# Context statistics, state products and reloaded results in other places of a two-layer DiT kernel, and the rotation on VectorE

## The chip, the cores and the metric

The kernel runs on one core of a Trainium2 chip. The metric is device time in microseconds (us) for one execution. TensorE (PE) does matrix products, VectorE (DVE), ScalarE (ACT) and GpSimd (POOL) do everything else on tiles, and SyncE (SP) issues most of the transfers between HBM and the on-chip memory. Each engine takes its own instructions in the order in which they were queued; between engines there are semaphores.

## The reference, cut to what matters

Two layers act on 512 rows `x` and 256 context rows `ctx`, each 2048 wide. Layer 0 (pooling and latent attention) isn't touched by the change. Layer 1 ("odd") is:

```
h, hc = rmsnorm(x)*(1+scale)+shift, rmsnorm(ctx)*(1+scale_c)+shift_c
mq,mk,mv,mo,mg,mz,aq,ak,av,az = split(h @ w_in)       # the same split of hc @ w_in for the context
state = mlstm_scan(context)                           # matrix memory: sums of w * v x k over the context
hm    = mlstm_scan(rows, state), forward and backward
ym    = rmsnorm(hm) * sigmoid(mo) * silu(mz)          # 4 heads of 256
q, k  = rope_2d(aq), rope_2d(ak)
ya    = window_attention(q, k, v, kc, vc, sink) * silu(az)   # 16 heads of 64, window 128, plus context
y     = concat(ym, ya) @ w_out
x     = x + gate * y ;  result = rmsnorm(x)
```

## The kernel before, in words

Everything is transposed: a tile holds 128 channels (partitions) by 512 rows or 256 context rows, so a 2048-wide value is 16 such tiles ("chunks", `j` = 0 to 15). Every operand of a product is split into a high and a low part in a rounded float type (`split`, line 107: a cast on ACT, line 108, then a subtraction on VectorE, line 109), and each product is three matmuls: high by high, high by low, low by high. Weights come in quarters of 128x1024 (`kq` = 0 to 3): `load_w` (line 111) issues the transfer from SP into one of three `wraw` buffers and splits it into four `wh` and four `wl` buffers, which is room for two quarters. `tmode` (line 299) and `kmode` (line 313) issue the matmuls of a quarter.

The order on the engines comes from a scheduling pass of the framework: it simulates the engines, and gives each one the earliest instruction in the source that is ready in that simulation. So the place in the source is a priority, not a position. Inside the blocks marked `manual_schedule` the order on PE is the order of the source, and some steps are marked `high_priority`.

The stages that the change touches:

- **Row statistics and the second layer's inputs** (lines 905 to 985). `stats1(v)` adds the squares of all chunks over the partitions with small matmuls (line 267 by way of `stat_mm`), takes the reciprocal root (`rstd_col`, lines 241 to 245), and spreads it with matmuls (`rows`, line 260). `h_chunk` (line 278) then makes the high and low parts of one chunk: a scaled product (line 289), an ACT step (line 291) and a VectorE step (line 292). For the rows these are the `HX` tiles (`hxh`, `hxl`), for the context the `HC` tiles (`hch`, `hcl`). In the source `stats1(1)` and the 16 context chunks stand ahead of both query groups of matrix memory (`x_group_t(6)` and `(7)`, 96 matmuls of 512 columns each, which read `HX` alone). The next group, which makes the first values and the gates, is the first that reads `HC`.
- **Context state** (lines 1199 to 1246). For each of the 4 heads `ctx_state` is a generator with two steps for each direction: scale the values (line 1219, VectorE) and split them (`wvh`, `wvl`); then six matmuls (line 1228) and a split of their result. One call starts it when a head's values are stored; two more calls come inside the next projection group, after its quarters 0 and 2. The background work that runs here on VectorE (`ada_vec_steps`, line 187) takes 128x512 blocks of a modulation weight from HBM.
- **Matrix memory** (line 1276 to 1435) makes eight result chunks (`z1d` 0 to 7, in HBM).
- **Windowed attention** (line 1440 to the end of the loop over heads). Its matmuls are interleaved by hand: a generator `fillers` yields one 512-column matmul at a time from the remaining projections (`w_proj(1)` to `w_proj(3)`: a query group and a gate group each) and then from the first three groups of the output projection (`out_steps`); `run(n)` takes n of them. `PRE`, `PRE2`, `PRE3` say how many are taken at the start, and `RATE` how many for each step of the attention. `wq_split` rotates a query tile (`do_rope`, line 329: a shuffle and a product on VectorE, a product on GpSimd at line 337, a sum on VectorE) and splits it. `Softmax.heads` (line 1511) takes scores for two heads: the masked maximum (line 1527), its scaled form against the sink (line 1528), the exponential (line 1529); `end` divides. `w_values` transposes the weights (line 1640), splits them (`wph`, `wpl`) and multiplies by the values (lines 1650 and 1651).
- **The result chunks** come back from HBM as `Z` tiles: `z_load(j)` (line 1558) loads two, casts them on VectorE (line 1563) and subtracts on GpSimd (line 1564). Their buffers lie in the same place as the `HX` tiles, whose pool is closed just before. All loads for the first output group stand inside `out_steps(0)`.

Of the kernel before, what the change touches and what calls it, by code (L numbers as in the profile page):

```python
# [8 lines left out]
F32 = mybir.dt.float32  # L9
F32R = mybir.dt.float32r  # L10
# [28 lines left out]
def tile_hybrid_dit(ctx: ExitStack, tc: tile.TileContext, ts: dict, out: bass.AP, dbg=None, upto=99):  # L39
# [286 lines left out]
        DM.dma_start(t, ts["rope"])  # L326
        return t[:, 0, :], t[:, 1, :]

    def do_rope(ps, r, tmp):

        sw = tmp("rsw", NX)
        t1 = tmp("rt1", NX)
        with tc.high_priority():
            V.stream_shuffle(sw, ps[:, :NX], SWAP)  # L334
            V.tensor_tensor(t1, ps[:, :NX], rope[0], op=ALU.mult)
        t2 = tmp("rt2", NX)
        G.tensor_tensor(t2, sw, rope[1], op=ALU.mult)
        V.tensor_tensor(r[:, :NX], t1, t2, op=ALU.add)

    def rtmp(pool, bufs=1):  # L340
        return lambda name, n: pool.tile([P, n], F32, name=name, tag=name, bufs=bufs)
# [597 lines left out]
    ezx.close()  # L939
    ehx, ehc, eht = (ExitStack() for _ in range(3))  # L940
    hxp = opool(ehx, "hx", side="right")
    HX = [(hxp.tile([P, NX], F32R, name=f"hxh{j}"), hxp.tile([P, NX], F32R, name=f"hxl{j}")) for j in range(KC)]
    bg.finish()
    stats1(0)

# [27 lines left out]
    hcp = opool(ehc, "hc", side="right")  # L973
    HC = [(hcp.tile([P, NC], F32R, name=f"hch{j}"), hcp.tile([P, NC], F32R, name=f"hcl{j}")) for j in range(KC)]
    htp = opool(eht, "htp")
    stats1(1)
    for j in range(KC):
        h_chunk(j, x1[j], ssq1, 12, 1, *((None, HC[j][i]) for i in range(2)), Ring(htp, 2), (1,))
    for i in range(2):
        for b, px in enumerate(x_group_t(G_MQ + i)):  # L980
            q = htp.tile([P, NX], F32, name="mqt", tag="mqt", bufs=2)
            S.mul(q, px, M_SCALE)
            G.dma_start(qxd[2 * i + b], q)
# [215 lines left out]
    def mv_group(h, state):  # L1199
        px, pc = new_px(2), new_pc()  # L1200
        pv = [px[b // 2][:, 256 * (b % 2) : 256 * (b % 2) + 256] for b in range(4)]
        for kq in range(4):
            w = load_w(odw[1 + h, kq])
            kcs = range(4 * kq, 4 * kq + 4)
            bg.step(2)
            kmode(pv, w, kcs, HX, kq == 0, kq == 3, 2)
            bg.step(3)
            kmode([pc[:, b, :] for b in range(2)], w, kcs, HC, kq == 0, kq == 3, 2)
            if kq % 2 == 0:
                next(state, None)  # L1210
        vx_store(h, [p_.rearrange("p (a b) -> p a b", b=256) for p_ in px])
        return vc_store([pc])
# [26 lines left out]
    for kq in range(4):  # L1239
        w = load_w(odw[5, kq])  # L1240
        bg.step(2)
        tmode(px, [pc[:, b, :] for b in range(2)], w, range(4 * kq, 4 * kq + 4), HX, HC, kq == 0, kq == 3)
        if kq % 2 == 0:
            next(state, None)
    bg.finish()
    ea.close()
# [210 lines left out]

    def wq_split(src):
        rr = ap2.tile([P, NX], F32, name="wrr", tag="wrr", bufs=1)
        do_rope(src, rr, rtmp(ap2))  # L1460
        res = []
        for a in range(2):
            own, oth = slice(64 * a, 64 * a + 64), slice(64 - 64 * a, 128 - 64 * a)
            q = ap2.tile([P, NX], F32R, name="wq", tag="wq", bufs=8)
            S.copy(q[own, :], rr[own, :])
            V.tensor_tensor(q[oth, :], rr[own, :], q[own, :], op=ALU.subtract)  # L1466
            res.append(q)
        return res
# [12 lines left out]
    def w_proj(i):  # L1481

        for g in (G_AQ + i, G_AZ + i):
            px = new_px2()
            if g < G_AZ:
                qs[i] = []
            else:
                zg[i] = ap2.tile([P, 2, NX], F32, name="wzg", tag="wzg", bufs=2)
            for kq in range(4):
                w = load_w(odw[g, kq])  # L1490
                kcs = range(4 * kq, 4 * kq + 4)
                for b in range(2):
                    yield from steps(px, w, kcs, (b,), HX, kq == 0, kq == 3)
                    if kq == 3 and g < G_AZ:
                        qs[i] += wq_split(px[b])
                    elif kq == 3:
                        S.activation(zg[i][:, b, :], px[b], AF.Silu)

    def w_bounds(nb):
        b0, b1 = max(0, nb - 1), min(4, nb + 2)  # L1500
# [2 lines left out]
    class Softmax:  # L1503
# [7 lines left out]
        def heads(self, pair):  # L1511
            i, nb = self.i, self.nb
            g = i // 2
            b0, b1, nl = w_bounds(nb)
            nk = nl + NC
            mk = (msk[:, P:], msk, msk, msk3)[nb]
            qq = slice(nb * P, (nb + 1) * P)
            ss_ = [new_w2() for _ in pair]
            for a, s in zip(pair, ss_):
                q = qs[i][a][:, qq]  # L1520
                for n, K in enumerate((KHw[g], KLw[g])):
                    T.matmul(s[:, 512 - nl : 512], q, K[:, b0 * P : b1 * P], start=n == 0, stop=n == 1)  # L1522
                    T.matmul(s[:, 512:768], q, K[:, NX:], start=n == 0, stop=n == 1)  # L1523
            for a, s in zip(pair, ss_):
                pr = wt("wpr_", 640)
                mx = tiny.tile([P, 1], F32, name="wm1", tag="wm1", bufs=4)
                V.tensor_tensor_reduce(pr[:, :nk], s[:, 512 - nl : 768], mk[:, :nk], 1.0, -3e38, ALU.add, ALU.max, mx)
                V.scalar_tensor_tensor(self.nmx[:, a : a + 1], mx, -A_SCALE, nsink[:, 4 * i + a : 4 * i + a + 1], op0=ALU.mult, op1=ALU.min)
                S.activation(pr[:, :nk], pr[:, :nk], AF.Exp, bias=self.nmx[:, a : a + 1], scale=A_SCALE, accum_out=self.ssm[:, a : a + 1])
                self.prs.append(pr)  # L1530

# [15 lines left out]
    def out_steps(g, px):  # L1547

        for kq in range(4):
            n = 4 - 2 * (kq == 3)  # L1550
            if g == 0:
                for j in range(4 * kq, 4 * kq + n, 2):
                    z_load(j)
            w = load_w(ts["od_out"][g, kq])
            yield from steps(px, w, range(4 * kq, 4 * kq + n), range(2), Z, kq == 0, False)
        ends.append((px, w[2:]))

    def z_load(j):
        raw = wp.tile([P, 1024], F32, name="wraw", tag="wraw", bufs=3)
        for i in range(2):  # L1560
            DM.dma_start(raw[:, 512 * i : 512 * i + 512], z1d[j + i])
            h, l = Z[j + i]
            V.tensor_copy(h, raw[:, 512 * i : 512 * i + 512])  # L1563
            G.tensor_tensor(l, raw[:, 512 * i : 512 * i + 512], h, op=ALU.subtract)

    def fillers():

        nonlocal Z, ezf
        for i in range(1, 4):
            yield from w_proj(i)  # L1570
        ehx.close()
        ezf = ExitStack()
        zp = opool(ezf, "zp1", side="right")
        Z = [(zp.tile([P, NX], F32R, name=f"z1h{j}"), zp.tile([P, NX], F32R, name=f"z1l{j}")) for j in range(KC)]
        pxs.append(new_px2())
        yield from out_steps(0, pxs[0])
        for g in (1, 2):
# [1 line left out]
            pxs.append([t[:, :512], t[:, 512:]])  # L1579
            yield from out_steps(g, pxs[g])  # L1580

    PRE, PRE2, PRE3, RATE, RATE_END = 16, 8, 20, 9.5, 13
    Z = ezf = None
    pxs, ends = [], []
    fill = fillers()

# [182 lines left out]
        stat_mm(p6[:, :2], ssq2[:, sl], 2, D, True, False)  # L1769
        finish(sl, out_evac(7, px, sl), p6)  # L1770
    eF.close()
    ezf.close()
    esP.close()


# [128 lines left out]
```

## Time and profile before

| | |
|---|---|
| median of 3 runs | 2305.13 us (2303.32 to 2306.37) |
| the profiled execution | 2305.76 us, of it 2304.0 us span between the first and the last instruction |
| granted TensorE clock, mean | 0.993 |
| busy: PE, VectorE, ACT, POOL | 2229.1, 1406.7, 916.3, 162.8 us |

PE is busy nearly all the time, so the profile is read by its exceptions: the list of waits of PE gives who ended each of its idle times (total, times, longest), and the table by stretches gives, for any piece of the span, how long each engine was busy and the share of the full clock that TensorE was granted in it (PEclk). A timeline line gives the start, the length, engine, line, what is written and read, and, in brackets, how long the engine was idle before and who ended that.

### The profile page before, as it was taken

What the parts mean: (1) busy time and instruction counts of PE and PEld (TensorE: products, weight loads), DVE (VectorE), ACT (ScalarE), POOL (GpSimd) and SP (SyncE); (2) the same over time, 40 slices, a digit from 0 to 9 for tenths busy, and PEclk for the clock granted to TensorE, in tenths of its full rate; (3) what the DMA queues carried; (4) which work ended last, traced back from release to release, by engine and by line L of the source; (5) the groups of instructions that cost most, each with busy time, mean ns of one, the idle gap of its engine ahead of it and who ended that gap; (6) DMA issues with size and microseconds to landing.
All of it is one profiled execution on the core that took longest, in us unless ns stands there. A gap on an engine that the chain in (4) does not pass through costs nothing. (4 is left out here: it accounts for less than half of the span.)

```text
span 2304.0 us, 34221 instructions
## 1 busy us (share of the span) xinstructions
PE 2229.1 (97%) x13000; PEld 1894.9 (82%) x13000; DVE 1406.7 (61%) x2841; ACT 916.3 (40%) x1864; POOL 162.8 (7%) x203
## 2 busy tenths in 40 slices
PE   5999999999999999999999999999999999999998
PEld 3678888788899999888888799988888878777887
DVE  5579523296666666788558524763455587778434
ACT  4232222112444444542226322223556667656432
POOL 0000100000000000011113100000000000003110
PEclk9999999999999999999999999999999999999999
DMA  9855323565211112276444321753232312113433
GB/s 386 322 202 179 121 85 115 185 227 186 100 49 54 51 56 69 101 252 224 160 158 154 93 100 65 247 185 120 88 101 94 103 61 68 65 55 122 135 113 116
DMA packets 118005, 309.14 MB, mean 134 GB/s; under 512 B 13612, under 2 KB 21292, under 8 KB 117840
## 3 DMA queue, kind: packets, MB, share of 16 engines
q1 hardware_dynamic: 110960, 279.64, 36.2%
q0 software_dynamic: 6880, 27.32, 3.2%
q8 instruction: 102, 1.67, 0.3%
q14 instruction: 63, 0.52, 0.1%
HBM read 277.28 MB, written 29.62 MB: 133 GB/s over the span
## 5 line engine op out<-in xcount | busy, mean ns | idle before, releaser
L108 ACT CAST wh<-wraw 128x512 fp32r<-128x512 f32 (+2 forms) x540 | 316.1, 590 | 852.5 <-PE pc L311 372.1
L109 DVE TENSOR_TENSOR wl<-wraw,wh 128x512 fp32r<-128x512 f32 (+2 forms) x540 | 358.5, 669 | 467.7 <-ACT wh L108 464.4
L187 DVE SCALAR_TENSOR_TENSOR acc<-at,st,acc 128x512 f32<-128x512 f32 x360 | 251.9, 749 | 25.8 <-DMA at<-in_ada_dram 24.2
L322 PE MATMUL px<-wh,hxh 128*128 128x512 f32 (+2 forms) x512 | 174.9, 342 | 0.8 <-ACT sz L1310 0.8
L322 PE MATMUL px<-wl,hxh 128*128 128x512 f32 (+2 forms) x512 | 174.0, 340 | 0.0
L322 PE MATMUL px<-wh,hxl 128*128 128x512 f32 (+2 forms) x512 | 173.9, 340 | 0.0
L309 PE MATMUL px<-h0h,wh 128*128 128x512 f32 x384 | 152.9, 398 | 0.0
L309 PE MATMUL px<-h0h,wl 128*128 128x512 f32 x384 | 151.7, 395 | 0.3 <-DVE wl L109 0.3
L309 PE MATMUL px<-h0l,wh 128*128 128x512 f32 x384 | 151.6, 395 | 0.0
L311 PE MATMUL pc<-h0h,wl 128*128 128x256 f32 x400 | 112.7, 282 | 0.0
L311 PE MATMUL pc<-h0h,wh 128*128 128x256 f32 x400 | 112.5, 281 | 0.0
L311 PE MATMUL pc<-h0l,wh 128*128 128x256 f32 x400 | 112.4, 281 | 0.0
L322 PEld LDWEIGHTS px<-wh,hxh 128*128 128x128 f32 x512 | 96.7, 189 | 13.6 <-ACT sz L1310 1.9
L322 PEld LDWEIGHTS px<-wl,hxh 128*128 128x128 f32 x512 | 96.7, 189 | 11.2
L322 PEld LDWEIGHTS px<-wh,hxl 128*128 128x128 f32 x512 | 96.6, 189 | 11.2
L309 PEld LDWEIGHTS px<-h0h,wh 128*128 128x128 f32 x384 | 72.1, 188 | 22.9 <-ACT wh L108 4.2
L309 PE MATMUL px<-hxh,wh 128*128 128x512 f32 x224 | 89.7, 400 | 0.0
L309 PE MATMUL px<-zxl,wh 128*128 128x512 f32 x224 | 89.3, 399 | 0.0
L309 PE MATMUL px<-hxl,wh 128*128 128x512 f32 x224 | 89.2, 398 | 0.0
L309 PE MATMUL px<-hxh,wl 128*128 128x512 f32 x224 | 89.1, 398 | 0.0
L309 PE MATMUL px<-zxh,wl 128*128 128x512 f32 x224 | 88.7, 396 | 0.0
L309 PE MATMUL px<-zxh,wh 128*128 128x512 f32 x224 | 88.2, 394 | 0.0
(887 smaller groups left out, 6010.1 us busy)
## 6 DMA issues: line engine op xcount, KB each, us to landing
at<-in_ada_dram SPq DMA_DIRECT2D x256, 256.0 KB, 3.4
at<-in_ada_dram SPq DMA_DIRECT2D x64, 512.0 KB, 7.9
wraw<-in_od_in_dram SPq DMA_DIRECT2D x64, 512.0 KB, 3.5
wraw<-in_ev_in_dram SPq DMA_DIRECT2D x56, 512.0 KB, 4.2
wraw<-in_ev_out_dram SPq DMA_DIRECT2D x44, 512.0 KB, 3.9
wraw<-in_od_oz_dram SPq DMA_DIRECT2D x32, 512.0 KB, 3.5
wraw<-in_od_out_dram SPq DMA_DIRECT2D x32, 512.0 KB, 3.5
xt<-in_xT_dram SPq DMA_DIRECT2D x16, 384.0 KB, 7.3
```

What stands on the lines that cost most here:

```text
L108: S.copy(h, src)
L109: low.tensor_tensor(l, src, h, op=ALU.subtract)
L187: V.scalar_tensor_tensor(a, at, st[:, kc, v : v + 1], a, op0=ALU.mult, op1=ALU.add)
L309: T.matmul(px[b], w_, Hx[kc][r_], start=s0, stop=s1)
L311: T.matmul(pc[b], w_, Hc[kc][r_], start=s0 and b == 0, stop=s1, skip_group_check=True)
L322: T.matmul(p_, h_, w_, start=s0, stop=s1, skip_group_check=True)
```

## The change

Seven edits, none of which changes what is computed:

1. `stats1(1)` and the 16 context chunks stand behind the first query group's matmuls in the source, and ahead of its evacuation.
2. The steps of `ctx_state` come after quarters 1 and 3 of the next group in place of 0 and 2.
3. Each `HX` tile has a tag of its own, and `z_place(j)` puts the `Z` tile of the same number there, one by one. The four loads of chunks 0 to 7 are issued during the last gate group of `w_proj`, two chunks after each of four of its steps; chunks 8 to 13 stay in `out_steps(0)`.
4. `z_load` splits like everything else: the cast on ACT, the subtraction on VectorE.
5. `wq_split` has the second product of the rotation on VectorE in place of GpSimd (8 calls; the rotations elsewhere stay as they were).
6. A gate group's first half is copied out and gets its `Silu` together with the second half.
7. In `heads` the two maxima come first, and one instruction of two columns takes the place of two at line 1528. `PRE2` and `PRE3` go from 8 and 20 to 16 and 12.

```
-    def do_rope(ps, r, tmp):
+    def do_rope(ps, r, tmp, eng=G):
...
-        G.tensor_tensor(t2, sw, rope[1], op=ALU.mult)
+        eng.tensor_tensor(t2, sw, rope[1], op=ALU.mult)
...
-    HX = [(hxp.tile([P, NX], F32R, name=f"hxh{j}"), hxp.tile([P, NX], F32R, name=f"hxl{j}")) for j in range(KC)]
+    HX = [tuple(hxp.tile([P, NX], F32R, name=f"hx{n}{j}", tag=f"hx{n}{j}") for n in "hl") for j in range(KC)]
...
-    stats1(1)
-    for j in range(KC):
-        h_chunk(j, x1[j], ssq1, 12, 1, *((None, HC[j][i]) for i in range(2)), Ring(htp, 2), (1,))
     for i in range(2):
-        for b, px in enumerate(x_group_t(G_MQ + i)):
+        pxs = x_group_t(G_MQ + i)
+        if i == 0:
+            stats1(1)
+            for j in range(KC):
+                h_chunk(j, x1[j], ssq1, 12, 1, *((None, HC[j][n]) for n in range(2)), Ring(htp, 2), (1,))
+        for b, px in enumerate(pxs):
...
-            if kq % 2 == 0:
+            if kq % 2:
                 next(state, None)
...
-        do_rope(src, rr, rtmp(ap2))
+        do_rope(src, rr, rtmp(ap2), V)
...
+                    elif kq == 3 and b == 0:
+                        S.copy(zg[i][:, 0, :], px[0])
                     elif kq == 3:
-                        S.activation(zg[i][:, b, :], px[b], AF.Silu)
+                        S.activation(zg[i][:, 1, :], px[1], AF.Silu)
+                        S.activation(zg[i][:, 0, :], zg[i][:, 0, :], AF.Silu)
+                    if g == G_AZ + 3 and 3 <= 2 * kq + b < 7:
+                        z_load(2 * (2 * kq + b - 3))
...
-            for a, s in zip(pair, ss_):
-                pr = wt("wpr_", 640)
-                mx = tiny.tile([P, 1], F32, name="wm1", tag="wm1", bufs=4)
-                V.tensor_tensor_reduce(pr[:, :nk], s[:, 512 - nl : 768], mk[:, :nk], 1.0, -3e38, ALU.add, ALU.max, mx)
-                V.scalar_tensor_tensor(self.nmx[:, a : a + 1], mx, -A_SCALE, nsink[:, 4 * i + a : 4 * i + a + 1], op0=ALU.mult, op1=ALU.min)
+            mx = tiny.tile([P, 2], F32, name="wm1", tag="wm1", bufs=2)
+            prs = [wt("wpr_", 640) for _ in pair]
+            for n, s in enumerate(ss_):
+                V.tensor_tensor_reduce(prs[n][:, :nk], s[:, 512 - nl : 768], mk[:, :nk], 1.0, -3e38, ALU.add, ALU.max, mx[:, n : n + 1])
+            a = pair[0]
+            V.scalar_tensor_tensor(self.nmx[:, a : a + 2], mx, -A_SCALE, nsink[:, 4 * i + a : 4 * i + a + 2], op0=ALU.mult, op1=ALU.min)
+            for a, pr in zip(pair, prs):
                 S.activation(pr[:, :nk], pr[:, :nk], AF.Exp, bias=self.nmx[:, a : a + 1], scale=A_SCALE, accum_out=self.ssm[:, a : a + 1])
...
-                for j in range(4 * kq, 4 * kq + n, 2):
+                for j in range(max(8, 4 * kq), 4 * kq + n, 2):
                     z_load(j)
...
             DM.dma_start(raw[:, 512 * i : 512 * i + 512], z1d[j + i])
-            h, l = Z[j + i]
-            V.tensor_copy(h, raw[:, 512 * i : 512 * i + 512])
-            G.tensor_tensor(l, raw[:, 512 * i : 512 * i + 512], h, op=ALU.subtract)
+            z_place(j + i)
+            split(raw[:, 512 * i : 512 * i + 512], *Z[j + i])
+
+    def z_place(j):
+
+        Z[j] = tuple(hxp.tile([P, NX], F32R, name=f"z1{n}{j}", tag=f"hx{n}{j}") for n in "hl")
...
-        ehx.close()
-        ezf = ExitStack()
-        zp = opool(ezf, "zp1", side="right")
-        Z = [(zp.tile([P, NX], F32R, name=f"z1h{j}"), zp.tile([P, NX], F32R, name=f"z1l{j}")) for j in range(KC)]
+        for j in (14, 15):
+            z_place(j)
...
-    PRE, PRE2, PRE3, RATE, RATE_END = 16, 8, 20, 9.5, 13
-    Z = ezf = None
+    PRE, PRE2, PRE3, RATE, RATE_END = 16, 16, 12, 9.5, 13
+    Z = [None] * KC
```

More of the change, by code (lines that the diff above doesn't have):

```diff
@@ L1242, in tile_hybrid_dit @@
         tmode(px, [pc[:, b, :] for b in range(2)], w, range(4 * kq, 4 * kq + 4), HX, HC, kq == 0, kq == 3)
-        if kq % 2 == 0:
+        if kq % 2:
             next(state, None)
@@ L1561, in z_load @@
             DM.dma_start(raw[:, 512 * i : 512 * i + 512], z1d[j + i])
-            h, l = Z[j + i]
-            V.tensor_copy(h, raw[:, 512 * i : 512 * i + 512])
-            G.tensor_tensor(l, raw[:, 512 * i : 512 * i + 512], h, op=ALU.subtract)
+            z_place(j + i)
+            split(raw[:, 512 * i : 512 * i + 512], *Z[j + i])
+    def z_place(j):
+        Z[j] = tuple(hxp.tile([P, NX], F32R, name=f"z1{n}{j}", tag=f"hx{n}{j}") for n in "hl")
     def fillers():
-        nonlocal Z, ezf
         for i in range(1, 4):
             yield from w_proj(i)
-        ehx.close()
-        ezf = ExitStack()
-        zp = opool(ezf, "zp1", side="right")
-        Z = [(zp.tile([P, NX], F32R, name=f"z1h{j}"), zp.tile([P, NX], F32R, name=f"z1l{j}")) for j in range(KC)]
+        for j in (14, 15):
+            z_place(j)
         pxs.append(new_px2())
@@ L1771, in tile_hybrid_dit @@
     eF.close()
-    ezf.close()
+    ehx.close()
     esP.close()
```

## The prediction, as it was put on record

> **What bounds the kernel now.** I read the busy times first, then the list of what PE waited for, then the table by stretches around the longest waits.
>
> ```profile
> span 2304.0 us, 34221 instructions
> ...
> PE 2229.1 (97%) x13000; PEld 1894.9 (82%) x13000; DVE 1406.7 (61%) x2841; ACT 916.3 (40%) x1864; POOL 162.8 (7%) x203
> ```
>
> PE is busy 97% of the span and the change leaves its matmuls as they are. So the change is worth what it does to the time in which PE stands still or runs below its clock. Of PE's waits, these lie at lines that the change touches (total, times, longest):
>
> ```profile
> PE wpo L1651 <- DVE wpl L109: 5.1, 6, 1.3
> PE ps6b L267 <- DVE ssq L891: 4.6, 2, 4.4
> PE pc L1228 <- ACT wvh L108: 3.9, 1, 3.9
> ...
> PE s L1522 <- DVE wm L1527: 2.1, 2, 1.9
> ...
> PE px L1478 <- ACT wzg L1497: 0.9, 1, 0.9
> ...
> PE pc L1228 <- DVE wvl L109: 0.8, 1, 0.8
> ```
>
> Two are single long ones: the context's statistics (4.4 us) and one head's state product (3.9 and 0.8). The rest is spread over windowed attention. The stretches show what the waits cost besides. The columns are the stretch, its length, then busy time of PE, PEld, DVE, ACT and POOL, the granted clock, DMA share, GB/s:
>
> ```profile
> 1269.00:1275.00 6.00, 1.58 (x8) 1.13 (x6) 3.41 (x4) 1.79 (x5) 2.02 (x2) 0.74 0.58 197
> 1275.00:1280.00 5.00, 5.00 (x18) 4.14 (x18) 2.18 (x8) 0.20 (x1) 0.00 (x0) 0.63 0.01 3
> 1280.00:1300.00 20.00, 20.00 (x88) 16.09 (x87) 18.29 (x53) 12.51 (x26) 2.09 (x4) 1.00 0.37 107
> 1504.00:1508.00 4.00, 3.88 (x20) 3.88 (x21) 3.33 (x7) 1.00 (x2) 0.00 (x0) 0.57 0.93 311
> 2044.00:2050.00 6.00, 5.92 (x18) 4.78 (x19) 5.81 (x17) 3.58 (x8) 0.00 (x0) 0.50 0.01 3
> ```
>
> After each long wait PE works on, but at 0.63, 0.57 and 0.50 of its clock. 5 us at 0.63 cost 1.85 us, 4 us at 0.57 cost 1.7, and 6 us at 0.50 cost 3.0. The third of these follows only the 1.9 us wait on `wm`.
>
> [...]
>
> **The change part by part.**
>
> *Context statistics.* Nothing is removed; the small matmuls, the spreading and 16 chunks get a lower priority than the 96 matmuls of the first query group.
>
> ```profile
> 1272.59 0.48 DVE L882 SCALAR_TENSOR_TENSOR x<-pc,av,xr 128x256 f32<-128x256 f32 x1 [1.02 <-DMA xr<-in_xT_dram]
> ```
> ```profile
> L982 ACT ACTIVATE mqt<-px x4: 577/598/601, 1285.4 to 1308.4; 128x512 f32<-128x512 f32 x4
> ```
> ```profile
> L292 DVE SCALAR_TENSOR_TENSOR hcl<-ht,av,hch x16: 471/480/485, 1281.3 to 1298.2; 128x256 fp32r<-128x256 f32 x16
> ```
>
> The sum of squares is late because the last context chunk's residual lands late (1272.6). When PE stood still at about 1269.5 the first query group wasn't done: its evacuation starts at 1285.4, so some 10 us of matmuls were left after 1275, or 8 at full clock. They now carry PE to about 1278, past the sum's end at about 1274 (the step at 1272.59 and two more). The wait goes, 4.4 us, and with it the slow clock after it: 1.85 us and half of the 0.8 us between 1274.2 and 1275. **-6.6 us.** What is late next: the chunks, now done from 1281.3 to 1298.7, come some 4 us later; their first reader stands behind the second query group, 96 matmuls at 0.227 us (88 in 20 us), so not before 1300, and the last chunk is read after seven more quarters of weights. The evacuations behind them on ACT (with their POOL transfers) release accumulators that nobody asks for before 1300. The danger is VectorE, busy 18.29 of 20 us in 1280 to 1300: a delayed weight half would be a new wait. Bounds: 0 (the scheduler still finds a gap for the statistics in the group) and -6.6.
>
> *Context state.* Each of the steps (0.61 us of scaling, 0.62 on ACT, 0.69 on VectorE, six matmuls, two splits) comes a quarter later. One wait is at stake:
>
> ```profile
> 1498.09 1.54 DVE L187 SCALAR_TENSOR_TENSOR acc<-at,st,acc 128x512 f32<-128x512 f32 x2 [3.83 <-DMA at<-in_ada_dram]
> ...
> 1501.59 0.61 DVE L1219 TENSOR_SCALAR wv<-vcx,wcol 128x258 f32<-128x258 f32 x2
> ...
> 1503.38 0.69 DVE L109 TENSOR_TENSOR wvl<-wv,wvh 128x516 fp32r<-128x516 f32 x1
> ```
> ```profile
> 1502.24 0.62 ACT L108 CAST wvh<-wv 128x516 fp32r<-128x516 f32 x1 [10.47 <-DVE wv L1219]
> 1502.77 1.14 ACT L108 CAST wh<-wraw 128x512 fp32r<-128x512 f32 x2
> ```
>
> Background work stood in VectorE's queue waiting 3.83 us for its weights, ahead of the scaling; `wvl` was ready at 1504.1, PE had wanted it at 1498.7. A quarter is 72 matmuls of 256 columns, at half of 0.227 us some 8.2 us, so PE now asks at about 1507, 3 us after. The two waits go (4.7 us) with the slow clock (1.7): **-6.4 us.** Behind the waiting cast on ACT stand two weight casts, done at 1503.9; the quarter that needs them starts at 1507. The second direction now ends with the group, and has the next quarter and a half as cover. Bounds: 0 and -6.4.
>
> *Result chunks.* 14 casts and 14 subtractions move from VectorE and GpSimd to ACT and VectorE; 8 pairs go into the group before. SP gets eight transfers ahead of later weight loads, through the same three raw buffers; in return they no longer stand two loads to each weight quarter in the first output group.
>
> ```profile
> L1563 DVE CAST z1h<-wraw x14: 411/421/1534, 2082.2 to 2110.0; 128x512 fp32r<-128x512 f32 x14
> L1564 POOL TENSOR_TENSOR z1l<-wraw,z1h x14: 1287/1444/1812, 2082.8 to 2111.5; 128x512 fp32r<-128x512 f32 x14
> ```
> ```profile
> 2060.00:2082.00 22.00, 22.00 (x123) 18.57 (x122) 16.35 (x45) 15.57 (x29) 1.12 (x2) 1.00 0.21 72
> 2082.00:2098.00 16.00, 12.84 (x61) 8.95 (x60) 15.27 (x24) 9.15 (x17) 12.49 (x9) 1.00 0.41 132
> 2098.00:2115.00 17.00, 14.66 (x73) 10.91 (x72) 15.42 (x35) 11.53 (x23) 7.25 (x5) 1.00 0.44 142
> ```
>
> A cast takes 0.42 us, but up to 1.53 next to a GpSimd subtraction. In 2082 to 2115 PE lacks 3.16 + 2.34 = 5.5 us, while VectorE is full (30.7 of 33 us) of stretched casts; `wpl` waits in its queue and PE for it. Afterwards six subtractions of 0.69 remain there (the price of `wvl` above), and no GpSimd operation. I take **-5.0 us** of the 5.5; bounds 0 and -5.5. The price is ahead of that: 8 subtractions (5.5 us) and 8 casts at the 0.62 of `wvh` (5.0 us) fall into about 2062 to 2082, where VectorE has 5.65 us free and ACT 6.4. That just fits.
>
> *Gate groups.* The table loads (`L1497` and the exponentials' return) cost this:
>
> ```profile
> L1497 ACT ACT_TABLE_LOAD x5 | 6.4, 1283 | 0.1
> ```
>
> Five loads for three groups become three, and two returns go: 4 x 1.28 = 5.1 us of ACT, less three copies of about 0.6. PE's one wait on `wzg`: **-0.9 us** (bounds 0 and -0.9).
>
> *Rotation.* Eight GpSimd products become VectorE products of about 0.69 us.
>
> ```profile
> 2041.52 1.27 POOL L337 TENSOR_TENSOR rt<-rsw,rope 128x512 f32<-128x512 f32 x1 [4.40 <-DVE rsw L334]
> ```
> ```profile
> 2041.86 1.21 DVE L1659 TENSOR_TENSOR wzt<-wzt,wzg 128x256 f32<-128x256 f32 x1
> ```
> ```profile
> 2097.98 0.42 DVE L1659 TENSOR_TENSOR wzt<-wzt,wzg 128x256 f32<-128x256 f32 x1
> ```
>
> The VectorE product at 2041.86 ends just after the GpSimd one; the same line takes 0.42 at 2097.98, so 0.8 us are lost in its shadow, about what the added product takes. So **0** for the wait on `wm` behind it. Bounds: +1.4 (0.69 at two such places, if nothing else shortens) and -4.9 (that wait and its slow clock both go).
>
> *Scores.* 32 of the 64 instructions at line 1528 go from VectorE, where no wait of PE in the list hangs on them. The first exponential of a pair now waits for the second maximum, but `end` needs all four anyway: 0, covered by the several steps of attention between a block's scores and its transposes. Moving eight fillers from behind the second pair to ahead of it is not free:
>
> ```profile
> 1864.49 0.40 PE L1478 MATMUL px<-hxh,wh 128*128 128x512 f32 x1
> ...
> 1869.16 0.27 PE L1640 MATMUL wpt<-con,wpr__18845 128*128 128x128 f32 x1
> ```
> ```profile
> 1868.73 0.71 ACT L1543 ACTIVATE wpr__18878<-wpr__18878,wr 128x512 f32<-128x512 f32 x1
> ```
>
> 20 fillers took 4.67 us (0.233 each), and the softmax ended at 1869.44, just in time for the transposes. With 12 fillers PE arrives 1.87 us sooner relative to the scores; the chain is a little shorter as less stands in its way. **+1.6 us**, bounds 0 and +1.9.
>
> Sum: -6.6 - 6.4 - 5.0 - 0.9 + 0 + 1.6 = -17.3 us. The profiled execution took 2305.76 (span 2304.0 and 1.8 around it), 0.6 above the median of the runs, so 2288.5 there and about **2288 us** as a median.
>
> **The rivals.** *Better:* the stretched operation and the longer chain through GpSimd were what made the 1.9 us wait; it goes with its slow clock (-4.9), and the start costs nothing (-1.6): 2281.5. For it: the third slow stretch hangs on one short wait. Against it: the product's 0.69 us stands in the same queue. *VectorE binds in windowed attention:* eight pairs and the rotations fill 2060 to 2082, so waits on `wpl` move there; nothing is left of -5.9, and the rotations cost +1.4: -6.6 - 6.4 + 1.4 + 1.6 = -10.0, 2295. For it: 16.35 + 5.5 of 22 us before anything waits. *The moved steps don't move:* priority isn't position, and the scheduler may put statistics and state where they were: -5.0 - 0.9 + 1.6 = -4.3, 2301. *Slower:* ACT takes its queue in order, and a chunk's cast can stand there waiting for its transfer with `wph` behind it and PE behind that. That ACT can stand so is shown by `wvh`: 10.47 us with two weight casts behind it. If each of the seven loads held ACT as long as that transfer held VectorE at 1498 (3.83 us, of which about 1 us is hidden), they would cost 7 x 2.8 = 20 us against -13.0 + 1.6 and no gain in the window: +8.5, 2313.5. It decides from (11.4 + 4.6) / 7 = 2.3 us a load. Against it: the casts have half a group's lead.
>
> [...]
>
> **How the numbers follow.** Forecast 0.48, better 0.24, VectorE binds 0.17, not moved 0.06, slower 0.05. A difference of 0.2% (4.6 us) is about what a measurement of this kernel can tell from none. The first three are faster by more (0.89), the fourth is within it (0.06), the last is slower (0.05). The range takes in the first three with the bounds of the unknown terms: 2277 (better, with the last 0.5 us of the chunks and about 4 us of the small waits in between) to 2298 (VectorE binds, with 3 us of one of the long waits coming back).
>
> **What would show it.** Right: no wait on `ssq` at line 267 and none at line 1228; the clock at 1.00 from 1240 to 1600; no GpSimd product at line 1564, casts of `z1h` on ACT near 0.6 us, and PE idle for less than 1 us over the first output group; one table load for each gate group; a new wait of 1 to 2 us at the first transposes of line 1640. Wrong: the long waits reappearing under another name (weight halves, `hcl`), waits on `wpl` during the last gate group, ACT idle ahead of `z1h` for a transfer, or a matmul row below full clock where it wasn't.

## The result, and the profile after

The changed kernel takes 2295.89 us (median of 6 runs, 2290.3 to 2296.3). The kernel before, run beside it, takes 2305.81 us (6 runs, 2303.32 to 2309.93). The ratio is 0.995 with a 95% interval of 0.9937 to 0.9963, that is 8.5 to 14.5 us less; the medians stand 9.9 us apart. The forecast was 17.3 us less, in a range from 2277 to 2298.

The changed kernel's page, as shown of before:

```profile
span 2294.0 us, 34184 instructions
...
PE 2222.4 (97%) x13000; PEld 1887.6 (82%) x13000; DVE 1398.1 (61%) x2817; ACT 922.6 (40%) x1881; POOL 131.8 (6%) x181
```

PE's busy time fell by 6.7 us although its matmuls are the same 13000: that is slow clock that went, and 3.1 of it went at two places in the first 1220 us that the change doesn't touch (at 43 and at 985 us the kernel before has 4 us at 0.57 in this execution). The rest is waits. The changed kernel's list of what PE waited for (total, times, longest), at the lines of the change; line numbers behind the moved pieces stand up to 9 higher than before:

```profile
PE s L1529 <- DVE wm L1534: 5.4, 2, 3.2
PE px L1480 <- ACT wzg L1501: 2.9, 2, 1.5
PE px L322 <- DVE wl L109: 2.8, 3, 1.6
...
PE wpt L1649 <- DVE wpr__18846 L1554: 1.0, 1, 1.0
...
PE ps6b L267 <- DVE ssq L891: 0.4, 1, 0.4
...
PE wpo L1660 <- DVE wpl L109: 0.2, 1, 0.2
```

The waits of 4.4 us on `ssq`, of 3.9 and 0.8 at the state product and of 5.1 on `wpl` are gone or nearly. Of those that grew, three are the largest: `wm` from 2.1 to 5.4, `wzg` from 0.9 to 2.9, and line 322 on `wl` is new with 2.8. The table by stretches of the changed kernel (stretch, length, busy PE, PEld, DVE, ACT, POOL, granted clock, DMA share, GB/s) shows the clock at the three places of before:

```profile
1269.00:1280.00 11.00, 11.00 (x49) 8.85 (x48) 8.41 (x14) 5.84 (x11) 2.45 (x2) 1.00 0.44 130
1500.00:1508.00 8.00, 8.00 (x69) 7.84 (x69) 6.16 (x12) 2.14 (x4) 0.00 (x0) 1.00 0.80 264
2034.00:2037.00 3.00, 1.02 (x9) 0.81 (x7) 2.96 (x5) 1.00 (x2) 0.00 (x0) 1.00 0.00 0
2037.00:2040.00 3.00, 1.81 (x6) 1.69 (x7) 2.99 (x9) 1.25 (x3) 0.00 (x0) 0.51 0.02 5
2040.00:2044.00 4.00, 4.00 (x11) 2.88 (x10) 2.52 (x5) 1.40 (x4) 0.00 (x0) 0.51 0.00 0
```

Two of the three slow stretches are gone. The third stays: PE stands still for most of 2034 to 2038, with a wait of 3.17 us on `wm` that ends at 2038.19, and from 2037 on its clock is 0.51 for some 7 us.

To see which stage gained how much, the same matmuls are compared in both traces. In the views of single tiles the last two times are the start of the first and of the last instruction of a group. Before:

```profile
L267 PE MATMUL ps6b<-od,ssq x12: 243/250/352, 1220.8 to 1274.9; 128*128 128x1 f32 x12
...
L322 PE MATMUL pc<-wh,hch x192: 277/280/385, 1311.1 to 1532.4; 128*128 128x256 f32 x160, 128*128 128x272 f32 x32
...
L311 PE MATMUL pc<-hch,wh x32: 278/280/283, 1532.9 to 1567.3; 128*128 128x256 f32 x32
...
L1478 PE MATMUL px<-z1h,wh x32: 387/395/480, 2083.2 to 2170.3; 128*128 128x512 f32 x32
...
L1651 PE MATMUL wpo<-wpl,vhl x72: 392/396/452, 1873.1 to 2150.2; 128*64 128x512 f32 x72
```

After:

```profile
L267 PE MATMUL ps6b<-od,ssq x12: 165/250/250, 1223.9 to 1281.4; 128*128 128x1 f32 x12
...
L322 PE MATMUL pc<-wh,hch x192: 277/280/385, 1307.4 to 1524.5; 128*128 128x256 f32 x160, 128*128 128x272 f32 x32
...
L311 PE MATMUL pc<-hch,wh x32: 278/280/283, 1525.8 to 1560.2; 128*128 128x256 f32 x32
...
L1480 PE MATMUL px<-z1h,wh x32: 389/395/502, 2078.2 to 2159.3; 128*128 128x512 f32 x32
...
L1660 PE MATMUL wpo<-wpl,vhl x72: 389/400/608, 1866.9 to 2139.3; 128*64 128x512 f32 x72
```

| stage | before | after | difference |
|---|---|---|---|
| start to the first `ps6b` (nothing changed there) | 1220.8 | 1223.9 | +3.1 |
| to the first context chunk `hch` (statistics) | 90.3 | 83.5 | -6.8 |
| to the last `hch` (state products) | 256.2 | 252.8 | -3.4 |
| to the first `z1h` (matrix memory, then most of windowed attention) | 515.9 | 518.0 | +2.1 |
| to the last `wpo` (reloaded results) | 67.0 | 61.1 | -5.9 |
| to the end | 153.8 | 154.7 | +0.9 |

The four stages in between gained 14.0 us in this pair of executions; the unchanged first 1220 us lost 3.1 and the end 0.9. That 3.1 isn't the change's: over the experiments below, whose source is the same up to there, the first `ps6b` starts between 1218.9 and 1227.3. So a stage is read from the traces, and a kernel's worth from its medians.

### The profile page after: what moved, and what is told of

The parts are those of the page before. It is cut to its first block, busy times and chain, and to the rows that moved or that the text cites. A ratio compares the mean times of both kernels' runs of the same rounds, so it can differ in the third digit from the quotient of the medians.

```text
span 2294.0 us, 34184 instructions
## 1 busy us (share of the span) xinstructions
PE 2222.4 (97%) x13000; PEld 1887.6 (82%) x13000; DVE 1398.1 (61%) x2817; ACT 922.6 (40%) x1881; POOL 131.8 (6%) x181
## 4 chain that ended last, share of the span: by engine, by line
PE 83%; DVE 7%; issue 4%; DMA 3%; ACT 2%; POOL 0%; SPq 0%; DVEq 0%; POOLq 0%; ACTq 0%
PE px L309 28%; PE pc L311 9%; PE px L322 8%; PE px L1480 5%; PE pj L645 5%; PE s L708 4%; PE om L751 2%; PE px L381 2%; PE s L1480 2%; DMA at<-in_ada_dram 2%; PE pc L322 2%; PE pj L665 2%; PE tp L733 2%; PE pa L143 1%; PE po L1393 1%
```

## The experiments

The theory after the result: each moved piece does its work, and what is missing was taken at three places in two queues. In VectorE's queue the weight halves stand behind background sums, and the maxima behind the rotation; on ScalarE the gate's two halves were torn apart by the exponentials. The rival: the parts disturb each other, and alone each would bring what the forecast gave it. Each kernel was timed beside the kernel before, 4 to 11 times (4 for one Silu and for each of the last two); the medians of the kernel before were 2305 to 2307 us. Two ratios of the changed kernel and its variants are told apart only where their intervals don't overlap.

| kernel | ratio to before | 95% interval | median, us |
|---|---|---|---|
| before + statistics moved | 0.9972 | 0.9962 to 0.9982 | 2297.95 |
| before + state steps moved | 0.9995 | 0.9986 to 1.0003 | 2303.59 |
| before + reload of results | 0.9977 | 0.9969 to 0.9986 | 2299.74 |
| before + rotation on VectorE | 1.0001 | 0.9992 to 1.0010 | 2304.93 |
| changed, rotation's product back on GpSimd | 0.9950 | 0.9936 to 0.9964 | 2294.50 |
| changed, one Silu | 0.9914 | 0.9901 to 0.9927 | 2286.02 |
| changed, 8 and 20 fillers | 0.9936 | 0.9922 to 0.9951 | 2291.35 |
| changed, six background buffers | 0.9928 | 0.9915 to 0.9941 | 2289.05 |
| changed, maxima at high priority | 0.9934 | 0.9921 to 0.9946 | 2290.61 |
| changed, gates as before | 0.9935 | 0.9922 to 0.9947 | 2292.14 |
| one Silu + six buffers + 8 and 20 | 0.9904 | 0.9889 to 0.9919 | 2285.80 |
| the same + rotation's end later | 0.9865 | 0.9848 to 0.9882 | 2274.93 |

**Statistics alone.** Only the lines of `stats1(1)` and its chunks move behind `x_group_t`, as in the diff above.

> The kernel before with the context's statistics alone moved behind the matmuls of the first query group. Theory: the wait of 4.4 us on `ssq` and the slow clock behind it go, -6.6 us, and the first chunk `hch` comes earlier by as much. Rival: the group's matmuls are only drawn forward and are missing later, where the second query group would wait for weight halves: -2 us or less. In the trace of the changed kernel the place gained 6.7 us; it is to be seen whether that stays when nothing else is changed.

The ratio gives 6.5 us less (4.1 to 8.8), and in its trace the first `hch` comes 6.6 us earlier, counted from the first `ps6b` (83.7 against 90.3). The theory holds: the step was worth what was forecast.

**State steps alone.**

```
-            if kq % 2 == 0:
+            if kq % 2:
                 next(state, None)
```

> The kernel before with the context's state steps alone moved one quarter later. Theory, as the prediction had it: both waits at the state matmul and the slow clock go and nothing takes their place, -6.4 us; then the 2.8 us on `wl` in the changed kernel come from another part of the change. Rival: the move itself makes the matrix unit wait for the low weight halves, which stand in VectorE's queue behind background sums that wait for their weights: -3.4 us, with about 3 us of waits of line 322 on `wl` between 1490 and 1520.

The ratio gives 1.2 us less (3.2 less to 0.7 more). From the list of PE's waits of this kernel, and then its table by stretches:

```profile
PE px L322 <- DVE wl L109: 3.8, 3, 2.1
```

```profile
1521.00:1525.00 4.00, 3.64 (x18) 3.64 (x19) 3.93 (x8) 0.00 (x0) 0.00 (x0) 0.57 0.81 248
```

Both waits at the state product are gone, but 3.8 us on low weight halves are there in their place, with a slow stretch of their own. The new wait belongs to the move itself. The rival written down holds in kind, though its 3.4 us lie just outside the interval, and the forecast's -6.4 falls.

**Reload alone.** The buffers of the rows are reused (`tag=f"hx{n}{j}"`), `z_load` splits on ScalarE and VectorE, and eight chunks go ahead of the first output group.

> The kernel before with the reload of matrix memory's results alone: into the rows' buffers, casts on ScalarE and subtractions on VectorE, eight chunks ahead of the first output group. Theory: 5 to 6 us less (the changed kernel gained 5.9 between the first `z1h` and the last `wpo`), and the waits on `wpl` fall from 5.1 us to under 1. Rival: VectorE is then overfull in the group before, so that `wpl` waits move there and only 2 us or less are left.

The ratio gives 5.3 us less (3.2 to 7.1), and between the first `z1h` and the last `wpo` its trace gained 6.8. From the list of PE's waits of this kernel:

```profile
PE wpo L1653 <- DVE wpl L109: 1.6, 3, 1.2
```

The theory holds in the gain; `wpl` fell from 5.1 us to 1.6 and not to under 1. Of the 1.6 only 0.2 stand beside the reload; the rest lies before 2040, where this edit changes nothing. The waits on `wpl` didn't move into the group ahead (2040 to 2084): this kernel's list has none there and 0.2 us in the changed one.

**Rotation alone.**

```
-        do_rope(src, rr, rtmp(ap2))
+        do_rope(src, rr, rtmp(ap2), V)
```

> The kernel before with the rotation's second product alone on VectorE. Theory, as the prediction had it: 0, within 1 us, since the product is as long as what VectorE loses beside GpSimd. Rival: the product and the sum behind it now stand ahead of the second maximum in VectorE's queue, as the trace of the changed kernel shows; the waits of line 1522 on `wm` grow from 2.1 to 4 to 5.5 us and the time by 2 to 3 us.

No difference (1.8 less to 2.3 more). The list of PE's waits of this kernel:

```profile
PE s L1522 <- DVE wm L1527: 5.8, 3, 3.3
...
PE wpo L1651 <- DVE wpl L109: 3.9, 4, 1.3
...
PE px L1478 <- DVE wl L109: 1.5, 1, 1.5
```

Both sides were half right: the time as in the theory, the cause as in the rival. The waits on `wm` grew by 3.7 us, as the rival had it, and one of 1.5 on a weight half came. Against these 5.2 us the wait of 2.0 on `az`, those of 1.7 on `wzt` and 1.2 of those on `wpl` went, 4.9 in all. The zero is a balance, not the absence of a cost. The changed kernel's VectorE timeline (start, length, engine, line) shows how the wait comes about:

```profile
1964.85 0.68 DVE L338 TENSOR_TENSOR wrr<-rt,rt 128x512 f32<-128x512 f32 x1
...
1966.33 0.69 DVE L1534 CUSTOM_DVE_ANT_0 wpr__19999<-s,msk 128x512 f32<-128x512 f32 x1
...
1967.06 1.39 DVE L1468 TENSOR_TENSOR wq<-wrr,wq 64x512 fp32r<-64x512 f32 x2
...
1969.40 0.68 DVE L1534 CUSTOM_DVE_ANT_0 wpr__20000<-s,msk 128x512 f32<-128x512 f32 x1
```

The two maxima of a pair belong together, but the rotation's low halves `wq` (1.39 us), a gating product and a `wpl` stand between them. The second maximum starts 3.1 us after the first, and PE starts the next scores only behind it, at 1970.23, after a wait of 2.19 us on `wm`.

**Rotation back on GpSimd, rest as changed.** The last argument `V` is dropped again.

> The changed kernel with the rotation's second product back on GpSimd. Theory, from the rotation alone (which measured no difference because a wait on `wm` 3.7 us longer stood against waits on `az`, `wpl` and `wzt` that were 5 us shorter): the waits on `wm` fall from 5.4 to about 2.1 us, those on `az` and `wzt` come back with about 3 us, and the time stays within 2 us of the 2295.9 of the changed kernel. Rival: in the changed kernel, where the reload no longer uses GpSimd, the other waits stay away, and the kernel becomes about 3 us faster, 2293.

The same time as the changed kernel (0.9950 both). From its list of PE's waits:

```profile
PE s L1529 <- DVE wm L1534: 2.4, 2, 1.9
...
PE s L1529 <- ACT az L1438: 2.2, 1, 2.2
...
PE wpo L1659 <- DVE wzt L1667: 1.7, 2, 1.0
```

`wm` is back at 2.4, `az` and `wzt` are back with 3.9. The theory holds in the trace; the rival's 3 us less lie at the edge of the interval, but the waits that it needs to stay away came back.

**One Silu over both halves.**

```
-                    elif kq == 3 and b == 0:
-                        S.copy(zg[i][:, 0, :], px[0])
                     elif kq == 3:
-                        S.activation(zg[i][:, 1, :], px[1], AF.Silu)
-                        S.activation(zg[i][:, 0, :], zg[i][:, 0, :], AF.Silu)
+                        S.copy(zg[i][:, b, :], px[b])
+                        if b:
+                            S.activation(zg[i], zg[i], AF.Silu)
```

> The changed kernel with both halves of a gate group copied out and one Silu over both (1024 columns), so that no order of the queue can put an exponential between the halves. Theory: the second table load goes, and the two waits on `wzg` of 1.5 and 1.3 us with it: 2.5 to 2.9 us less, 2293. Rival: the copy of the second half stands just as late in ScalarE's queue and the waits keep their length: no difference, or the gate comes so late that line 1667 waits for it.

It is 8.3 us faster than the changed kernel by the difference of the two ratios (0.9914 against 0.9950; the intervals don't touch), more than the theory gave. The groups of ACT instructions (busy, mean ns of one, idle before) of the changed kernel, then of this one:

```profile
L1538 ACT ACT_TABLE_LOAD x6 | 7.7, 1283 | 0.1
...
L1502 ACT ACT_TABLE_LOAD x3 | 3.8, 1283 | 0.1
...
L1501 ACT ACT_TABLE_LOAD x2 | 2.6, 1283 | 0.0
```

```profile
L1537 ACT ACT_TABLE_LOAD x4 | 5.1, 1283 | 0.1
...
L1501 ACT ACT_TABLE_LOAD x3 | 3.8, 1283 | 0.1
...
L1501 ACT ACTIVATE wzg<-wzg 128x1024 f32<-128x1024 f32 x3 | 3.2, 1061 | 0.0
```

In the changed kernel the loads for the gates are still five and those for the exponentials six: of two Silus the scheduler ran the one on the copied half as soon as it could, then exponentials, then the other. With one Silu there are three and four, the saving that the forecast had counted, and no wait on `wzg` is left. The other part in the traces is clock, in a stretch that nothing in this edit touches directly (the table by stretches of this kernel):

```profile
2029.00:2033.00 4.00, 1.05 (x9) 0.84 (x7) 3.95 (x7) 1.05 (x2) 0.00 (x0) 1.00 0.00 0
2033.00:2036.00 3.00, 2.76 (x14) 2.39 (x15) 3.00 (x10) 2.17 (x6) 0.00 (x0) 1.00 0.02 5
```

The same wait of 3.2 us on `wm` stands here, and no slow stretch follows: up to 2044 the clock stays at 1.00. That makes 2.9 us of waits and 2.9 of clock in the traces (half clock from 2037.1 to 2043.9, with PE busy for 5.7 of it); the last 2.5 us of the difference are within the intervals. The part of the clock I take for luck and no merit of the edit: behind this wait of 3.2 or 3.3 us the clock was 0.51 in the changed kernel, 0.52 (2045.6 to 2049) with the rotation alone and 1.00 here, and the last section sets such places side by side.

**Gates as before, rest as changed.** Each half's Silu reads the accumulator, without a copy.

> The changed kernel with the gates as before: each half's Silu straight out of the accumulator, no copy. Theory: the change's own form costs what the waits on `wzg` grew by, 2.9 less 0.9: 2 us less, 2294. Rival: with the rest of the change in place the form before would wait as long, since ScalarE now also has the casts of the reloaded chunks: 0, and the second wait (1.3 us beside the reload) stays.

0.9935 against 0.9950 for the changed kernel: 3.5 us in the direction of the theory, but the intervals overlap. In its trace the waits on `wzg` are 1.4 us against 2.9. So the change's own form of the gates cost 1.5 us of waits, by this pair of traces, where the forecast had a gain of 0.9.

**8 and 20 fillers again.** `PRE2, PRE3 = 8, 20`.

> The changed kernel with 8 fillers between the first and the second pair of the first block and 20 behind the second, as before the change. Theory, as the prediction had it: 1.6 us less, by the waits of 1.0 and 0.2 us on the first transposes of line 1649 (bounds 0 and 1.9); the wait of 1.6 us of line 1624 lies ahead of the moved fillers and stays. Rival: the wait only moves to the second pair's scores, which then stand eight matmuls earlier: 0.

0.9936, with overlapping intervals again. In the trace the first transposes of line 1649 wait 0.3 and 0.2 us in place of 1.0 and 0.2, and line 1624 waits 1.3 in place of 1.6. Theory and trace agree in sign; the size (0.7 to 1.0 against 1.6) can't be told from the medians.

**Six buffers for the background weights.**

```
-    bg = Background(range(20, 24), pp, opool(ea, "ada1"), 4, "atr", 1)
+    bg = Background(range(20, 24), pp, opool(ea, "ada1"), 6, "atr", 1)
```

> The changed kernel with six buffers in place of four for the weights of the background sums behind the context's state. Theory: the waits of line 322 on `wl` come from background sums that stand in VectorE's queue waiting for those weights; two more buffers let the transfers run ahead, the waits fall from 2.8 us to under 1 and the time by 2 to 3 us. Rival: the sums are held by the state step's own scaling and casts in the queues, or the transfers by their bandwidth (0.93 of the DMA engines were busy there): the waits stay and the time with them.

5.1 us faster than the changed kernel (0.9928 against 0.9950; the intervals overlap between 0.9937 and 0.9941). The same stretch of 30 us, in the changed kernel and then in this one:

```profile
1490.00:1520.00 30.00, 27.24 (x227) 26.48 (x227) 24.81 (x44) 5.05 (x9) 0.00 (x0) 1.00 0.78 254
```

```profile
1490.00:1520.00 30.00, 30.00 (x259) 29.84 (x257) 26.54 (x46) 5.41 (x10) 0.00 (x0) 1.00 0.74 252
```

PE lacks 2.76 us in the first and nothing in the second; no wait of line 322 on `wl` is left. The VectorE timeline of the changed kernel shows what the buffers removed. In brackets stands how long VectorE was idle and for what:

```profile
1512.54 0.75 DVE L187 SCALAR_TENSOR_TENSOR acc<-at,st,acc 128x512 f32<-128x512 f32 x1 [0.59 <-DMA at<-in_ada_dram]
1513.51 0.75 DVE L187 SCALAR_TENSOR_TENSOR acc<-at,st,acc 128x512 f32<-128x512 f32 x1 [0.22 <-DMA at<-in_ada_dram]
1515.03 0.75 DVE L187 SCALAR_TENSOR_TENSOR acc<-at,st,acc 128x512 f32<-128x512 f32 x1 [0.76 <-DMA at<-in_ada_dram]
1515.70 0.68 DVE L109 TENSOR_TENSOR wl<-wraw,wh 128x512 fp32r<-128x512 f32 x1
```

VectorE stands idle 1.57 us for data that the waiting matmuls don't need, with the low weight half behind it. The theory holds by the traces, and the transfers' rate (0.74 of the DMA engines here, 0.78 in the changed kernel) wasn't the limit. Six buffers in the kernel before, with the state steps where they were, weren't run: since background sums that waited for their data also held the scaling there, the buffers might have done without the move.

**Maxima at high priority.** `with tc.high_priority():` around the two `tensor_tensor_reduce` of `heads`.

> The changed kernel with the maxima of the scores at high priority in the scheduler; at the first of the two places the second maximum then stands ahead of the rotation's sum in VectorE's queue, at the second the two maxima stand together behind it. Theory: the waits on `wm` of 5.4 us are the price of the product's place in the queue; the one of 2.2 us becomes about 1 and 1 to 4 us go, with the slow clock of 3.4 us (6.83 us at half) if a wait of under 2 us is too short for it. Rival: the maxima only push the rotation and its release of the accumulators back, and the waits appear on `px` instead: 0.

0.9934 against 0.9950, 3.7 us less, with overlapping intervals. From its list of PE's waits:

```profile
PE wpo L1660 <- DVE wzt L1668: 4.7, 4, 3.1
```

No wait on `wm` is left, but 4.7 us on `wzt`, which hardly was there before (0.6): now the gating stands behind the rotation. The rival's kind was right and its place wrong (`wzt`, not `px`); whether the time is the rival's 0 or in the theory's range, the medians can't tell. With that much queued something has to give way, and neither the maxima nor the gating may: what is left is the rotation.

**Three repairs together.**

> The changed kernel with one Silu over both halves, six buffers for the background weights, and 8 and 20 fillers around the second pair. Theory: the three act in different stages and add up: against the changed kernel 4.9 + 4.4 + 0.8, the steps that each showed in its own trace, so about 10 us less, 2286. Rival: part of what one Silu brought in the windowed stage was the slow clock that stayed away once (3.4 us) and comes back: 2289.

2285.80 us, ratio 0.9904, 10.6 us less than the changed kernel by the ratios, as expected. Against one Silu alone it is only 2.3 us less, with overlapping intervals, so the time by itself doesn't show that the three add up; the trace does for the six buffers (no wait of line 322 on `wl`) and the fillers (0.3 and 0.2 us at the first transposes). The mean granted clock was 0.995 in its profiled execution, against 0.996 in the changed kernel's, and a wait of 2.2 us on `wzt` is new. Its largest waits in the windowed stage:

```profile
PE s L1528 <- DVE wm L1533: 5.4, 2, 3.2
PE wpo L1658 <- DVE wzt L1666: 3.0, 2, 2.2
```

**The rotation's end later in the source.** The shuffle and the first product, which read the accumulator, stay; the second product, the sum and the low halves are issued 12 matmuls later:

```
                     yield from steps(px, w, kcs, (b,), HX, kq == 0, kq == 3)
+                    if late:
+                        qs[i] += late.pop()()
                     if kq == 3 and g < G_AZ:
-                        qs[i] += wq_split(px[b])
+                        late.append(wq_start(px[b]))
```

> The combination of one Silu, six buffers and 8 and 20 fillers, and besides the rotation's end (second product, sum, low halves) stands 12 matmuls later in the source than its beginning, so that the maxima of the scores and the gating lie ahead of it in VectorE's queue. Theory: the waits on `wm` (5.4 us) and the long ones on `wzt` (3.0) in the combination come from the rotation's place in VectorE's queue and not from its amount of work; they fall to under 3 us together, and the time from 2285.8 to about 2280. Rival: VectorE has no free time there wherever the rotation stands, the waits only change their names as with the maxima at high priority: within 2 us of 2285.8.

2274.93 us, ratio 0.9865: 9.0 us less than the three repairs by the ratios, 19.6 less than the changed kernel. From its list of PE's waits:

```profile
PE wpo L1676 <- DVE wzt L1684: 0.7, 1, 0.7
```

This is the only one left on either; there is none on `wm`, and the granted clock is 1.00 in each of three stretches from 1820 to 2118 us (0.97 in the changed kernel from 1960 to 2078). VectorE does the same work (1398.5 us against 1398.1 in the changed kernel). So the theory holds: it was the place in the queue, not the amount of work. Of the 9.0 us, 7.7 are waits on these two (5.4 and 3.0 less 0.7); the mean granted clock rose from 0.995 in the three repairs' profiled execution to 0.998.

## Why the prediction was right or wrong

The time came out inside the range, but 7 to 8 us above the forecast: two of the six terms failed, and what let the range hold was the room left for a rival.

*Statistics, -6.6.* Right in mechanism and size: -6.8 in the trace, -6.5 alone. The covering matmuls were there, and the chunks that come later kept nobody waiting.

*Context state, -6.4.* The step that failed is the one on cover: "Behind the waiting cast on ACT stand two weight casts, done at 1503.9; the quarter that needs them starts at 1507." It followed ScalarE's queue only. The low halves of the same weights stand in VectorE's queue behind the background sums, whose wait for their data the prediction had quoted itself (3.83 us). They became the next late thing: -3.4 in the trace, -1.2 alone. The answer to "what is late next" has to be looked for in every queue that the shifted consumer reads from.

*Result chunks, -5.0.* Right: -5.9 in the trace, -5.3 alone. VectorE's and ScalarE's free time ahead was enough; the first casts start at 2045.7, 32 us ahead of the first `z1h`, where the prediction had reckoned with 20.

*Gate groups, -0.9.* Wrong in mechanism. "Five loads for three groups become three" took order in the source for order on the engine. The scheduler put the exponentials between the two Silus; the loads stayed five, and the waits on `wzg` grew by 2.0 (1.5 of it undone by the old form). The same saving, made in one instruction, was real.

*Rotation, 0.* The number was right by luck, its reason was not. The added product doesn't merely replace lost time: it pushes the maxima back (+3.7 us of waits on `wm`), and frees `az`, `wzt` and `wpl` of about as much. The upper bound of +1.4 for the wait itself was too small, since with the product the sum and the low halves behind it fall between two maxima. The prediction also hung the third slow stretch on the 1.9 us wait alone. A wait of 0.97 us on `wzt` ended 1.1 us of matmuls earlier, and in the 3.41 us up to the slow clock PE was busy for only 1.14.

*Fillers, +1.6.* Right in place and sign: the new wait at line 1649 is 1.2 us, and 0.7 of it goes when the fillers go back.

*The sum.* The four parts that were run alone make -12.8 (6.5 + 1.2 + 5.3, less 0.2); with 2.0 for the gates and 1.2 for the first transposes that gives -9.6, against 9.9 measured by the medians and 11.5 by the ratio. So close a sum is partly chance, as each part is known to about 2 us at best, and the state step gained 3.4 in the changed kernel's trace against 1.2 alone. Against the forecast's 17.3 the state step lacks 5.2 us and the gates 2.9; the others together are 0.4 better than theirs. The time came out at that of the rival "VectorE binds in windowed attention" (2295), but not by its mechanism: that rival wanted the waits on `wpl` to move into the last gate group and the reload's gain to vanish, and neither happened. Only its smaller clause, a cost of the rotation in VectorE's queue, is seen. The rivals "moved steps don't move" and "slower" didn't show: the steps moved, and ACT stood 3.7 us in all for the reloaded chunks, with PE waiting 0.2 on `wpl`. Of the signs named for "Right", two failed: there is not one table load for each gate group, and over the first output group PE lacks 1.6 us and not under 1 (1.3 of it a wait on `wzg`).

The third slow stretch was counted as hanging on the wait on `wm`, and "Better" let both go together. The last experiment did just that, with another edit; but the two don't always go together, as the last section shows.

## What to carry to other kernels

When a step is moved away from a stall, follow each of the waiting engine's other inputs back through its own queue: the next stall can be a background instruction that waits for data of its own, and two buffers more took that stall away here. When two instructions must run side by side (two maxima, two uses of one table), make them one instruction, or give their neighbours a later place in the source, since the scheduler sees readiness and not pairs. A part that measures zero can be a gain and a loss; its trace shows the loss, and that can be removed by itself.

## What the runs showed of the hardware

In these traces the length of a wait alone doesn't give the granted clock. Behind the same wait of 3.2 us on `wm`, TensorE ran at 0.51 for 7 us in the changed kernel and at 1.00 from 2029 to 2044 with one Silu. At the earlier of the two places PE was busy for 1.72 of 4 us with the rotation alone and for 1.81 of 4 in the changed kernel (its wait of 2.2 us); in the next 4 us the clock was 0.57 and 1.00. The rotation alone, then the changed kernel:

```profile
1973.00:1977.00 4.00, 1.72 (x14) 1.50 (x13) 3.83 (x12) 1.61 (x5) 0.00 (x0) 1.00 0.00 0
1977.00:1981.00 4.00, 4.00 (x12) 3.00 (x12) 3.53 (x11) 2.81 (x8) 0.00 (x0) 0.57 0.31 105
```

```profile
1967.00:1971.00 4.00, 1.81 (x14) 1.61 (x13) 3.73 (x12) 0.98 (x3) 0.00 (x0) 1.00 0.00 0
1971.00:1975.00 4.00, 4.00 (x21) 3.23 (x20) 2.39 (x7) 3.83 (x11) 0.00 (x0) 1.00 0.35 126
```

The traces of the kernel before and of the changed kernel show how these stretches lie in time. Within each of the two, all changes of the clock lie whole multiples of 3.413 us apart: in the kernel before, for instance, at 1271.92, 1278.75, 1504.03, 1507.44, 2043.33 and 2050.16, in the changed kernel at 2037.08, 2043.91 and 2282.84. Where this grid lies against the program differs between the two: counted back to the first instruction, its first line stands at 2.2 us in the one and at 2.7 in the other. The four slow stretches that they have between 1240 and 2250 us are one or two windows of the grid long, 3.41 us once and 6.83 three times, at 0.50, and so cost at most 1.7 or 3.4 each. Below are windows of the grid. The first three rows are the kernel before, the next two the changed kernel at its waits of 3.2 and of 2.2 us, and the last two are stretches of the same length around the 3.2 us with one Silu. The third number is PE's busy time:

```profile
1268.51:1271.92 3.41, 1.31 (x6) 0.74 (x4) 2.82 (x3) 1.36 (x4) 2.42 (x2) 1.00 0.52 180
1500.61:1504.03 3.42, 0.38 (x1) 0.19 (x1) 3.38 (x8) 1.66 (x3) 0.00 (x0) 1.00 0.83 260
2039.92:2043.33 3.41, 1.14 (x6) 0.74 (x6) 3.36 (x7) 0.97 (x2) 1.27 (x1) 1.00 0.01 2
2033.67:2037.08 3.41, 1.35 (x10) 1.01 (x8) 3.36 (x6) 1.30 (x3) 0.00 (x0) 1.00 0.00 0
1968.81:1972.22 3.41, 1.99 (x11) 1.75 (x12) 3.20 (x11) 1.41 (x4) 0.00 (x0) 1.00 0.00 0
2028.12:2031.53 3.41, 1.93 (x13) 1.45 (x11) 3.37 (x8) 1.88 (x4) 0.00 (x0) 1.00 0.00 0
2031.53:2034.94 3.41, 1.70 (x10) 1.52 (x11) 3.40 (x10) 1.14 (x3) 0.00 (x0) 1.00 0.02 5
```

The first four were followed by half clock, the others not. With one Silu the 3.2 us fell half into one stretch and half into the next. In the kernel before and the changed kernel, between 1240 and 2250 us, the first four rows are all the windows at full clock in which PE was busy for less than 1.4 us; every other had 1.77 or more, and none of those was followed by half clock. This holds for this part of these two traces alone: at 981.79 in the kernel before half clock followed a window with 1.98 us. So a wait of 2 or 3 us had its slow stretch or not, in these traces, as the grid happened to cut it.

The mean clock differs between kernels accordingly: 0.993 in the profiled execution of before, 0.996 in the changed kernel's and 0.998 in the last one's. Counted only while PE was busy, the half clock cost 10.2 us in the first of these executions and 3.5 in the second. Of the 10.2, 3.1 lie in the first 1220 us, which no edit touches. So of the 31 us between the first and the last kernel's medians at most about 10 are clock and not waiting, by the first execution, and a third of these is chance.
